# Waiting by semaphore for products in GpSimd's DMA queue, and another order of the last products, in a hybrid stick-breaking and retention layer

## The chip, the cores and the metric

One NeuronCore of one Trainium2 chip runs the whole program. The metric is the device time of one execution in microseconds, the median of several runs. Engines are named as in the profile: PE (TensorE, matrix products), PEld (its weight loads), DVE (VectorE), ACT (ScalarE), POOL (GpSimd, which here mostly issues DMAs and masks tiles), SP (the sync engine, which issues DMAs only). Every engine works through a queue of its own in order.

## The reference

One inference step of a layer with two groups of eight heads. 1024 frames of a new stream (the prompt) and 8 x 16 frames of running streams (the sample) are normalised and projected, one head group attends by stick-breaking, the other by retention; both outputs are normalised by head, multiplied with a gate, and go through one output projection. What the change touches is the end of it, on the prompt's rows:

```python
y = jnp.concatenate([y_sb, y_r], axis=-1)          # 2048 wide, both head groups
out = jnp.einsum('bte,ed->btd', y, w_out)          # output projection, 2048 x 2048
x = x + rms_norm(out, norm_post)                   # out / rms(out) * norm_post, added to the input
```

Beside it stand the new keys and values and the retention states.

## The kernel before

The prompt's 1024 rows are handled in two groups of four tiles of 128 rows; group 0 also carries the 128 sample rows. For each group and head the kernel projects q, k, v and gates (`products`, `project_rows`, `project_both`, L310 to L406), each weight block being split into a high and a low part in a format that PE takes (`split`, L139: ACT rounds, DVE subtracts) and multiplied in three products. The attention of a head runs beside it as a job: scores, sigmoids (ACT), masks (POOL, `weights`, L602), a scan (DVE, L616), a turn through DRAM (`turn_out`, `turn_in`, L569 and L581), products with the values, and a last norm and gate (`finish`, L634), whose result goes to DRAM (s_y) and, for group 1, is added by an adding DMA into the row sums S1 (L659).

The output projection multiplies the rows of both groups with w_out by a scheme with seven products in place of eight for blocks of rows and columns (as in Strassen's method). It needs sums of rows (S1, S2, s3, s4; in DRAM, made by `row_sums`, L1243, with copies and adding DMAs from DRAM to DRAM on POOL's queue) and sums of columns of w_out (s_t, `column_sums`, L1223, by DVE). The table `STEPS` (L281) lists the 28 products of this stage, each of 4 tiles x 4 blocks x 3 = 48 matmuls; (2, "1") is product 1 of the third of four quarter passes. Tile t and column block c of the result are gathered in `outs[t][c]` by `give` (L1394), which at the last contribution squares on ACT (for the norm) and multiplies with norm_post on DVE. The first four tiles are finished by `finish_first` and stored by `send_first` while the last products run; the other four are finished one by one by `last_done`, each after its last product: `last_scale` works out the factor, `scale` multiplies by it and adds x, `send` stores. The sum with x has two forms: for some (t, c) (`added`, L1424) x was copied to y before (`give_x`, L1442, on ACT's queue), ACT scales, and an adding DMA on POOL's queue stores; for the others x is loaded (`load_x`, L1429, POOL's queue), DVE scales and adds, and a plain DMA stores, on POOL's queue for tiles 0 to 3 and on SP's for 4 to 7.

The order is set by jobs: `tick` (L172) is called after every projection matmul group and lets at most one job go on whose time has come, so waits in the code (`yield 12`) count products. `place` (L163) ties an instruction to the product just issued, for its place in the order only, without a semaphore: an engine whose queue reaches it early runs it early. `row_sums(0)` handles heads 0 to 3 while the heads of group 1 are still projected, `row_sums(1)` heads 4 to 7 during the output projection. `mixed_last` (L1318) runs the last two products of `STEPS`, (3, "7") and (3, "4"), tile by tile: "7" and at once "4" into the same PSUM bank.

Of the kernel before, what the change touches and what calls it, by code (L numbers as in the profile page):

```python
# [12 lines left out]
ALU = mybir.AluOpType  # L13
# [6 lines left out]
H = 8  # L20
# [3 lines left out]
PT = 8  # L24
# [39 lines left out]
def tile_hybrid_step(  # L64
# [26 lines left out]
    nc = tc.nc  # L91
# [16 lines left out]
    def x_rows(t):  # L108
        return x_prompt[0, t * P : (t + 1) * P, :] if t < PT else xs_flat
# [25 lines left out]
    s_sum = {n: scr.tile([P, H, 512], F32, name=f"s_{n}") for n in ("S1", "S2", "s3", "s4")}  # L135
# [22 lines left out]
    clock = [0]  # L158
    phase = [0]
    product = [None]  # L160
    AFTER = mybir.DependencyInfo(mybir.DependencyClass.NoSync, mybir.DependencyReason.DATA)

    def place(inst):  # L163
        if product[0] is not None:
            tc.add_manual_dep(inst.ins, product[0].ins.name, AFTER, reason="placed behind a product")

    class Job:
        def __init__(self, steps, after=0):
            self.steps, self.at, self.done = steps, clock[0] + after, False
            jobs.append(self)  # L170

    def tick():  # L172
        clock[0] += 1
        for job in jobs:
            if job.at <= clock[0]:
                wait = next(job.steps, None)
                jobs.remove(job)
                if wait is None:
                    job.done = True
                else:  # L180
                    job.at = clock[0] + wait
                    jobs.append(job)
                return
# [224 lines left out]
    with ExitStack() as s1:  # L408
# [49 lines left out]
        with tc.tile_pool(name="p0", bufs=2) as p0, tc.tile_pool(name="p0s", bufs=1) as p0s, tc.tile_pool(  # L458
            name="p0p", bufs=4, space=PSUM
# [164 lines left out]
        class Out:  # L624
# [5 lines left out]
            def done(self, i):  # L630
                sq = op.tile([P, P], F32, name="sq", tag="sq", bufs=1)
                nc.scalar.activation(sq, self.o[:, i, :], AF.Square, accum_out=self.ssq[:, i : i + 1])
# [610 lines left out]
        def row_sums(q, wait):  # L1243
            heads = range(q * H // 2, (q + 1) * H // 2)
            for name, first, more in (
                ("S2", lambda h: s_sum["S1"][:, h, :], lambda h: s_y[0][:, h, :NB_TOK]),
                ("s3", lambda h: s_y[0][:, h, :NB_TOK], lambda h: s_y[1][:, h, :]),
                ("s4", lambda h: s_sum["S2"][:, h, :], lambda h: s_y[0][:, H + h, :NB_TOK]),
            ):
                for act, src in ((nc.gpsimd.dma_start, first), (add_rows, more)):  # L1250
                    for h in heads:
                        if not ready[h]():
                            while not ready[h]():
                                yield 3
                            yield 48
                        place(act(s_sum[name][:, h, :], src(h)))
                        yield wait
                made.add((name, q))

        made = set()  # L1260
        ready = {}

        def add_rows(dst, src):
            return nc.gpsimd.dma_start(dst, src, accum_op=ALU.add)
# [31 lines left out]
        def mixed_step(name, k, p, bank, block, fresh=False):  # L1296
            hi, lo = mix[USES[name]]
            wh, wl = block
            ts = slice(p * P, (p + 1) * P)
            for n, (a, b) in enumerate(((hi, wh), (hi, wl), (lo, wh))):  # L1300
                product[0] = nc.tensor.matmul(  # L1301
                    bank, a[:, k, ts], b,
                    start=(fresh and k == 0 and n == 0), stop=(k == H // 2 - 1 and n == 2),
                    skip_group_check=True,
                )
                tick()
# [11 lines left out]
        def mixed_last(two, banks, done):  # L1318
            kept = [mp.tile([P, 4, 512], F32R, name=f"w{x}", tag=f"m{x}1") for x in "hl"]
            blocks = [list(mixed_blocks(keep=kept)), list(mixed_blocks())]  # L1320
            for p in range(4):
                for name, w in zip(two, blocks):
                    for k in range(H // 2):
                        mixed_step(name, k, p, banks[p], w[k])
                    done(name, p)

        for gi in range(2):
            if gi:
# [47 lines left out]
    with ExitStack() as s3:  # L1376
# [11 lines left out]
        gpost = c3.tile([P, D], F32, name="gpost")  # L1388
# [2 lines left out]
        given = {(t, c): 1 for t in range(4) for c in range(2)}  # L1391
        xrs = {}

        def give(t, c, bank):  # L1394
            o = outs[t][c]
            n = given[t, c] = given.get((t, c), 0) + 1
            end = n == (4 if t < 4 else {0: 3, 1: 5, 2: 2, 3: 4}[c])
            if n == 1:
                nc.scalar.activation(o, bank, AF.Copy)
            elif end and t >= 4:  # L1400
                nc.vector.scalar_tensor_tensor(o, bank, -1.0, o, ALU.mult, ALU.subtract)  # L1401
            else:
                nc.vector.tensor_tensor(o, bank, o, ALU.add)  # L1403
            if end:
                sq = rp.tile([P, 512], F32, name="sq3", tag="sq3")
                nc.scalar.activation(sq, o, AF.Square, accum_out=ssq[:, t, c : c + 1])
                nc.vector.tensor_tensor(o, o, gpost[:, c * 512 : (c + 1) * 512], ALU.mult)  # L1407

        def scale(t, c, rs):
            o = outs[t][c]  # L1410
            if added(t, c):
                nc.scalar.activation(o, o, AF.Copy, scale=rs)
            else:
                nc.vector.scalar_tensor_tensor(o, o, rs, xrs[t, c], ALU.mult, ALU.add)  # L1414

        def send(t, c):
            at = y_rows(t)[:, c * 512 : (c + 1) * 512]
# [4 lines left out]
            return (nc.gpsimd if t < 4 else nc.sync).dma_start(at, outs[t][c])  # L1422

        def added(t, c):  # L1424
            return c < (2 if 4 <= t < 7 else 1)

        wanted = [(t, c) for t in range(PT) for c in range(4) if not added(t, c)]

        def load_x(q):  # L1429
            for x in "hl":  # L1430
                xr = mp.tile([P, 5, 512], F32, name="xr", tag=f"m{x}{q}")
                for j in range(5):
                    if wanted:
                        t, c = wanted.pop(0)
                        place(nc.gpsimd.dma_start(xr[:, j], x_rows(t)[:, c * 512 : (c + 1) * 512]))
                        xrs[t, c] = xr[:, j]
                        yield 10

        xs_given = {}
        SYNC = mybir.DependencyInfo(mybir.DependencyClass.Sync, mybir.DependencyReason.DATA)  # L1440

        def give_x():  # L1442
            for t in range(PT):
                cs = slice(0, 1024 if added(t, 1) else 512)
                xs_given[t] = nc.scalar.dma_start(y_rows(t)[:, cs], x_rows(t)[:, cs])
                place(xs_given[t])
                yield 24
# [32 lines left out]
        def send_first():  # L1480
            for n in range(16):
                while len(scaled) <= n:
                    yield 2
                place(send(*scaled[n]))
                yield 12 if added(*scaled[n]) else 8

        def finish_sample():
# [16 lines left out]
        scaled = []  # L1504
# [3 lines left out]
        for step, (n, name) in enumerate(STEPS):  # L1508
# [28 lines left out]
            def last_done(name, p):  # L1537
                t = 4 + p
                c = {"7": x2, "4": x1}[name]
                give(t, c, banks[3, "1"][p])  # L1540
                if name == "7":
                    more_of(t, c)
                else:
                    u_ = last_scale(t, c)
                    for cc in (0, 1, 3, 2):
                        scale(t, cc, u_)
                        send(t, cc)
# [99 lines left out]
```

## Time and profile before

| | |
|---|---|
| median of 3 runs | 2324.88 us (2320.08, 2324.88, 2325.47) |
| the profiled execution | 2320.76 us, its span 2319.0 us |
| granted PE clock, mean over the span | 0.996 |
| busy: PE, DVE, ACT, POOL | 2271.0, 1418.3, 918.6, 629.1 us |
| DMA | 476.21 MB, mean 205 GB/s |

The span reaches from the first to the last instruction of the profiled execution; the time of that execution is 1.76 us longer. Lines of the profile name source line, engine, operation and output<-inputs with buffer numbers left out, so s_S stands for S1 and S2, s_s for s3 and s4. An entry like [5.05 <-DMA s_S<-sg] gives the engine's idle time ahead of the row and what ended it.

### The profile page before, as it was taken

How to read it: one execution, taken by the hardware profiler on the slowest of the kernel's cores; microseconds unless marked ns; L12 is line 12 of the kernel's file. 1: busy time of each engine (PE TensorE's matmuls, PEld its weight loads, DVE VectorE, ACT ScalarE, POOL GpSimd, SP SyncE). 2: the span in 40 equal slices, each digit the busy share in tenths (PEclk: the TensorE clock that was granted, in tenths of full speed). 3: DMA queues.
4: the chain of work that ended last, by engine and by line, in shares of the span. 5: the costliest groups of instructions: out<-in, count | busy, mean ns of one | idle time of the engine just before them, and what ended most of it. 6: DMA issues, size and time to landing. Idle time of an engine off the chain costs nothing. (4 is left out here: it accounts for less than half of the span.)

```text
span 2319.0 us, 38754 instructions
## 1 busy us (share of the span) xinstructions
PE 2271.0 (98%) x13920; PEld 2012.8 (87%) x13920; DVE 1418.3 (61%) x2770; ACT 918.6 (40%) x1896; POOL 629.1 (27%) x930
## 2 busy tenths in 40 slices
PE   7999999999999999999999999999899999999996
PEld 7999999999999999999888888888788888888884
DVE  8246564556555564555757767676566656756766
ACT  6323332323333242333443444454334444545343
POOL 2123241414224141322412322142323213131022
PEclk9999999999999999999999999999999999999998
DMA  7659787797869787798968788888888776787566
GB/s 253 153 142 226 172 182 182 178 208 158 201 161 198 179 187 179 163 227 216 224 193 253 219 241 239 238 246 247 231 237 199 207 189 179 233 274 245 176 207 174
DMA packets 701185, 476.21 MB, mean 205 GB/s; under 512 B 232416, under 2 KB 631008, under 8 KB 699200
## 3 DMA queue, kind: packets, MB, share of 16 engines
q1 hardware_dynamic: 615968, 309.71, 51.3%
q0 software_dynamic: 48672, 140.69, 23.6%
q10 hardware_dynamic: 36352, 23.34, 3.4%
q8 instruction: 109, 1.79, 0.3%
q14 instruction: 84, 0.69, 0.1%
HBM read 371.89 MB, written 117.18 MB: 211 GB/s over the span
## 5 line engine op out<-in xcount | busy, mean ns | idle before, releaser
L315 PE MATMUL acc<-mh,wh 128*128 128x256 f32 (+2 forms) x2304 | 660.8, 339 | 5.7 <-DVE rv L1166 5.7
L315 PE MATMUL acc<-ml,wh 128*128 128x256 f32 (+2 forms) x2304 | 661.7, 340 | 0.8 <-DVE p0u L153 0.8
L315 PE MATMUL acc<-mh,wl 128*128 128x256 f32 (+2 forms) x2304 | 662.5, 340 | 0.0
L141 DVE TENSOR_TENSOR wl<-wr,wh 128x512 fp32r<-128x512 f32 x432 | 296.8, 690 | 414.8 <-ACT wh L140 400.8
L140 ACT ACTIVATE wh<-wr 128x512 fp32r<-128x512 f32 x432 | 272.8, 632 | 601.1 <-PE acc L315 354.4
L315 PEld LDWEIGHTS acc<-mh,wh 128*128 128x128 f32 x2304 | 421.8, 188 | 41.7 <-issue 6.6
L315 PEld LDWEIGHTS acc<-ml,wh 128*128 128x128 f32 x2304 | 421.5, 188 | 36.0 <-issue 6.6
L315 PEld LDWEIGHTS acc<-mh,wl 128*128 128x128 f32 x2304 | 421.5, 188 | 35.9 <-issue 8.2
L764 POOL DMA_DIRECT2D kc<-cache_sb_k x256 | 166.5, 655 | 283.1 <-DVE kcT L795 131.2
L374 PE MATMUL accn<-whn,mh 128*128 128x256 f32 x768 | 224.0, 292 | 0.0
L374 PE MATMUL accn<-wln,mh 128*128 128x256 f32 x768 | 217.2, 283 | 0.0
L374 PE MATMUL accn<-whn,ml 128*128 128x256 f32 x768 | 217.1, 283 | 0.0
L374 PEld LDWEIGHTS accn<-whn,mh 128*128 128x128 f32 x768 | 146.7, 191 | 9.8 <-issue 7.9
L374 PEld LDWEIGHTS accn<-wln,mh 128*128 128x128 f32 x768 | 146.8, 191 | 0.3
L374 PEld LDWEIGHTS accn<-whn,ml 128*128 128x128 f32 x768 | 146.6, 191 | 0.0
L616 DVE TENSOR_TENSOR_SCAN kp<-kp 128x640 f32<-128x640 f32 (+6 forms) x72 | 108.5, 1507 | 45.9 <-POOL kp L605 43.4
L1301 PE MATMUL a<-wl,mh 128*128 128x512 f32 x320 | 125.0, 391 | 0.8 <-DVE wl L141 0.8
L1301 PE MATMUL a<-wh,ml 128*128 128x512 f32 x320 | 125.0, 391 | 0.0
L1301 PE MATMUL a<-wh,mh 128*128 128x512 f32 x320 | 124.3, 390 | 0.4 <-DVE o L1403 0.4
L575 POOL DMA_DIRECT2D s_o<-so x16 | 18.6, 1162 | 302.8 <-DVE kp L594 227.8
L588 DVE STREAM_TRANSPOSE kp<-be 128x640 f32<-128x640 f32 (+6 forms) x72 | 95.5, 1326 | 5.9 <-DMA be<-s_bd 5.9
L141 DVE TENSOR_TENSOR wln<-wrn,whn 128x512 fp32r<-128x512 f32 x80 | 55.0, 689 | 68.2 <-ACT whn L140 67.6
(269 smaller groups left out, 3691.6 us busy)
## 6 DMA issues: line engine op xcount, KB each, us to landing
wr<-w_in SPq DMA_DIRECT2D x384, 256.0 KB, 4.7
vc<-cache_sb_v SPq DMA_DIRECT2D x64, 512.0 KB, 7.3
wr<-w_out SPq DMA_DIRECT2D x112, 256.0 KB, 4.3
wrn<-w_in SPq DMA_DIRECT2D x80, 256.0 KB, 3.8
kc<-cache_sb_k SPq DMA_DIRECT2D x256, 64.0 KB, 4.1
kc<-cache_sb_k POOLq DMA_DIRECT2D x256, 64.0 KB, 4.5
tr<-w_out SPq DMA_DIRECT2D x32, 512.0 KB, 6.1
s_t<-ts POOLq DMA_DIRECT2D x64, 256.0 KB, 4.6
```

The source lines that it names most:

```text
L140: nc.scalar.activation(hi, src, AF.Copy)
L141: nc.vector.tensor_tensor(lo, src, hi.bitcast(F32), ALU.subtract)
L315: last = nc.tensor.matmul(a[:, :m], lhs[:, j, :], rhs[w][:, j, o : o + m], start=(w == 0 and j == 0 and n == 0), stop=(w == KT // WQ - 1 a ...
L374: product[0] = nc.tensor.matmul(a, lhs[q][:, jj, ts], rhs[:, j, :], start=(w == 0 and j == 0 and n == 0 and t % 2 == 0), stop=(w == KT // ...
L575: place(q.dma_start(s[c].rearrange("m q a -> q m a"), src[:, 32 * c.start : 32 * c.stop].rearrange("q (m a) -> q m a", a=32),))
L588: place(nc.vector.transpose(dst.rearrange("p (k b j) -> p k j b", j=4, b=32), raw))
L616: nc.vector.tensor_tensor_scan(rev, rev, rev, 1.0, ALU.mult, ALU.bypass)
L764: (nc.gpsimd if i < 2 else nc.sync).dma_start(kc[32 * i : 32 * i + 32, :].rearrange("p (k d) -> p k d", d=32), cache_k[0, 2 * c + j, s * 5 ...
L1301: product[0] = nc.tensor.matmul(bank, a[:, k, ts], b, start=(fresh and k == 0 and n == 0), stop=(k == H // 2 - 1 and n == 2), skip_group_c ...
```

## The change

Five things are edited. `pace` ties a DMA to a product with a semaphore, so that POOL waits until PE has run that product; `passed` keeps the product of every tick. It replaces `place` for the copies and adds of the row sums (a product 40 ticks back for heads 0 to 3, the last one for heads 4 to 7), for the loads of x and for the first stores. A head's rows are taken up 60 ticks after its end was first seen. The last products go in steps over two tiles. The last multiplication with norm_post of the products "4" writes the PSUM bank in place of the SBUF tile. Tiles 6 and 7 lose the adding form: all their column blocks are scaled on DVE and stored by SP, so 24 blocks of x are loaded in place of 21, and x is copied to y for six tiles in place of eight.

```diff
+    def pace(inst, back=0):
+        tc.add_manual_dep(inst.ins, passed[-1 - back].ins.name, SYNC, reason="paced by a product")
+        return inst
+
     def tick():
         clock[0] += 1
+        if product[0] is not None:
+            passed.append(product[0])
...
                     for h in heads:
-                        if not ready[h]():
-                            while not ready[h]():
-                                yield 3
-                            yield 48
-                        place(act(s_sum[name][:, h, :], src(h)))
+                        while not settled(h):
+                            yield 3
+                        pace(act(s_sum[name][:, h, :], src(h)), 40 if q == 0 else 0)
                         yield wait
...
+        since = {}
+
+        def settled(h):
+            for g in ready:
+                if ready[g]():
+                    since.setdefault(g, clock[0])
+            return h in since and clock[0] - since[h] >= 60
...
-            for p in range(4):
-                for name, w in zip(two, blocks):
-                    for k in range(H // 2):
-                        mixed_step(name, k, p, banks[p], w[k])
-                    done(name, p)
+            for p, q in ((0, None), (1, 0), (2, 1), (3, 2), (None, 3)):
+                for name, w, tile_at in zip(two, blocks, (p, q)):
+                    if tile_at is not None:
+                        for k in range(H // 2):
+                            mixed_step(name, k, tile_at, banks[tile_at], w[k])
+                        done(name, tile_at)
...
-                nc.vector.tensor_tensor(o, o, gpost[:, c * 512 : (c + 1) * 512], ALU.mult)
+                gained[t, c] = bank if to_bank else o
+                nc.vector.tensor_tensor(gained[t, c], o, gpost[:, c * 512 : (c + 1) * 512], ALU.mult)
...
-                nc.vector.scalar_tensor_tensor(o, o, rs, xrs[t, c], ALU.mult, ALU.add)
+                nc.vector.scalar_tensor_tensor(o, gained[t, c], rs, xrs[t, c], ALU.mult, ALU.add)
...
-            return c < (2 if 4 <= t < 7 else 1)
+            return c < {4: 2, 5: 2, 6: 0, 7: 0}.get(t, 1)
...
-                        place(nc.gpsimd.dma_start(xr[:, j], x_rows(t)[:, c * 512 : (c + 1) * 512]))
+                        pace(nc.gpsimd.dma_start(xr[:, j], x_rows(t)[:, c * 512 : (c + 1) * 512]))
...
-            for t in range(PT):
+            for t in range(6):
...
-                place(send(*scaled[n]))
+                pace(send(*scaled[n]))
...
-                give(t, c, banks[3, "1"][p])
+                give(t, c, banks[3, "1"][p], name == "4")
```

The first place is POOL's queue while the fifth head of group 1 is handled: AFFINE_SELECT are the masks of a row, s_be and be the way of a row through DRAM, s_t the column sums, and s_S_109<-s_S_108 the copy of head 3's rows from S1 to S2. Before:

```order
L659 DMA s_S_108<-sg 128x512
L582 DMA be<-s_be_4_18204 128x5x128
L1256 DMA s_S_109<-s_S_108 128x512
L605 AFFINE_SELECT kp<-kp 128x128
L605 AFFINE_SELECT be<-be 128x128
L1240 DMA s_t_107<-ts 128x512
L1220 DMA s_raw<-raw 128x512
L1240 DMA s_t_107<-ts 128x512
L575 DMA s_be_6_18445<-be 128x28x32
L1264 DMA s_S_109<-s_y_104 128x512
L582 DMA be<-s_be_5_18327 128x6x128
```

With the change:

```order
L668 DMA s_S_108<-sg 128x512
L591 DMA be<-s_be_4_18202 128x5x128
L614 AFFINE_SELECT kp<-kp 128x128
L614 AFFINE_SELECT be<-be 128x128
L1249 DMA s_t_107<-ts 128x512
L1263 DMA s_S_109<-s_S_108 128x512
L1229 DMA s_raw<-raw 128x512
L1249 DMA s_t_107<-ts 128x512
L584 DMA s_be_6_18445<-be 128x28x32
L591 DMA be<-s_be_5_18325 128x6x128
L1249 DMA s_t_107<-ts 128x512 x2
L1278 DMA s_S_109<-s_y_104 128x512
```

The copy stands one row behind the masks and a store of s_t in place of directly ahead of the masks, and the add of S2 (from s_y) stands behind the load of be and two stores, in place of ahead of them.

The second place is the end of PE's queue: a_23436 (before) is the bank of the last tile, a_23434 and a_23433 (with the change) the banks of the last tile and of the one ahead; wh and wl without a number are the weights of product "7", those with a number the first block of weights of "4". Before:

```order
L1301 MATMUL a_23436<-wh,s3h 128x512
L1301 MATMUL a_23436<-wl,s3h 128x512
L1301 MATMUL a_23436<-wh,s3l 128x512
L1301 MATMUL a_23436<-wh_24122,a22h 128x512
L1301 MATMUL a_23436<-wl_24123,a22h 128x512
L1301 MATMUL a_23436<-wh_24122,a22l 128x512
```

With the change:

```order
L1315 MATMUL a_23434<-wh,s3h 128x512
L1315 MATMUL a_23434<-wl,s3h 128x512
L1315 MATMUL a_23434<-wh,s3l 128x512
L1315 MATMUL a_23433<-wh_24123,a22h 128x512
L1315 MATMUL a_23433<-wl_24124,a22h 128x512
L1315 MATMUL a_23433<-wh_24123,a22l 128x512
```

Before, the first row of "4" (a22h) follows the last row of "7" in the same bank; now it goes into the bank of the tile ahead, and the last tile's "4" comes twelve rows later.

The third place is the end of DVE's queue, from the addition of the last product on (o_2 with a bank a). Before:

```order
L1401 SCALAR_TENSOR_TENSOR o_2_21911<-a_23436,o_2_21911 128x512
L1407 TENSOR_TENSOR o_2_21911<-o_2_21911,gpost 128x512
L1457 SCALAR_TENSOR_TENSOR most<-ssq_21942,most 128x1
L1464 RECIPROCAL lastr<-lastr 128x1
L1465 SCALAR_TENSOR_TENSOR lastu<-lastr,most 128x1
L1466 SCALAR_TENSOR_TENSOR lastu<-lastu,lastr 128x1
L1414 SCALAR_TENSOR_TENSOR o_1_21932<-o_1_21932,lastu,xr 128x512
L1414 SCALAR_TENSOR_TENSOR o_3_21919<-o_3_21919,lastu,xr 128x512
L1414 SCALAR_TENSOR_TENSOR o_2_21911<-o_2_21911,lastu,xr 128x512
```

With the change (five more rows follow it, the last of the factor and the four scalings of the last tile):

```order
L1418 SCALAR_TENSOR_TENSOR o_2_21911<-a_23434,o_2_21911 128x512
L1481 RECIPROCAL lastr<-lastr 128x1
L1425 TENSOR_TENSOR a_23434<-o_2_21911,gpost 128x512
L1482 SCALAR_TENSOR_TENSOR lastu<-lastr,most 128x1
L1474 SCALAR_TENSOR_TENSOR most<-ssq_21942,most 128x1
L1483 SCALAR_TENSOR_TENSOR lastu<-lastu,lastr 128x1
L1432 SCALAR_TENSOR_TENSOR o_0_21938<-o_0_21938,lastu,xr 128x512
L1432 SCALAR_TENSOR_TENSOR o_1_21931<-o_1_21931,lastu,xr 128x512
L1432 SCALAR_TENSOR_TENSOR o_3_21918<-o_3_21918,lastu,xr 128x512
L1432 SCALAR_TENSOR_TENSOR o_2_21910<-a_23433,lastu,xr 128x512
L1481 RECIPROCAL lastr<-lastr 128x1
L1482 SCALAR_TENSOR_TENSOR lastu<-lastr,most 128x1
```

Before, three scalings follow the last addition. Now the third tile's factor and its four scalings stand behind that addition too, ahead of the last tile's.

More of the change, by code (lines that the diff above doesn't have):

```diff
@@ L170, in __init__ @@
             jobs.append(self)
+    SYNC = mybir.DependencyInfo(mybir.DependencyClass.Sync, mybir.DependencyReason.DATA)
+    passed = []
+    def pace(inst, back=0):
+        tc.add_manual_dep(inst.ins, passed[-1 - back].ins.name, SYNC, reason="paced by a product")
+        return inst
     def tick():
         clock[0] += 1
+        if product[0] is not None:
+            passed.append(product[0])
         for job in jobs:
@@ L1392, in tile_hybrid_step, with give @@
         xrs = {}
-        def give(t, c, bank):
+        gained = {}
+        def give(t, c, bank, to_bank=False):
             o = outs[t][c]
@@ L1439, in tile_hybrid_step @@
         xs_given = {}
-        SYNC = mybir.DependencyInfo(mybir.DependencyClass.Sync, mybir.DependencyReason.DATA)
         def give_x():
-            for t in range(PT):
+            for t in range(6):
                 cs = slice(0, 1024 if added(t, 1) else 512)
```

## The prediction

> **What bounds the kernel now.** I read the stages first, then whom TensorE (PE) waits for, then the timeline at the two places found. In the table of stages the columns are the stretch in us, its length, busy us and instruction count of PE, PEld, DVE, ACT and POOL, the granted clock, the DMA share and GB/s.
>
> ```profile
> 1500.00:1600.00 100.00, 100.00 (x475) 83.79 (x474) 68.69 (x112) 46.46 (x90) 31.67 (x44) 1.00 0.86 248
> 1600.00:1700.00 100.00, 91.87 (x431) 76.33 (x430) 61.64 (x108) 39.80 (x84) 27.69 (x37) 0.97 0.87 241
> 1700.00:1800.00 100.00, 100.00 (x479) 83.77 (x478) 68.61 (x129) 44.15 (x92) 33.24 (x41) 1.00 0.80 208
> ...
> 2000.00:2100.00 100.00, 99.62 (x437) 81.69 (x436) 59.09 (x99) 46.72 (x73) 29.29 (x43) 1.00 0.88 271
> ...
> 2250.00:2300.00 50.00, 44.10 (x176) 33.69 (x177) 39.97 (x80) 23.94 (x56) 11.41 (x18) 0.97 0.50 143
> 2300.00:2306.00 6.00, 4.39 (x18) 2.93 (x16) 5.71 (x15) 3.85 (x9) 2.30 (x4) 1.00 1.09 205
> 2306.00:2319.00 13.00, 0.00 (x0) 0.00 (x0) 4.31 (x10) 1.90 (x5) 2.53 (x3) 0.61 0.87 208
> ```
>
> PE is the bound: the stages around 1600 to 1700 are full. Time can only come from where PE stands still: 8.13 us in 1600 to 1700, 5.90 + 1.61 us in 2250 to 2306, and 13.0 us after its last product. The two longest of PE's waits there, in the view of whom it waits for (total us, times, longest):
>
> ```profile
> PE acc L315 <- DVE rv L1166: 5.7, 1, 5.7
> ...
> PE accx L402 <- DVE wlx L141: 1.7, 1, 1.7
> ```
>
> **The stall near 1650.** Three rows of POOL, one of DVE, one of PE, in order of cause; the bracket holds the idle time ahead and its releaser.
>
> ```profile
> 1624.21 0.93 POOL L659 DMA_DIRECT2D s_S<-sg  x1
> ...
> 1631.08 0.57 POOL L1256 DMA_DIRECT2D s_S<-s_S  x1 [5.05 <-DMA s_S<-sg]
> 1631.65 0.31 POOL L605 TENSOR_SCALAR_AFFINE_SELECT kp<-kp 128x128 f32<-128x128 f32 x1
> 1631.99 2.09 DVE L616 TENSOR_TENSOR_SCAN kp<-kp 128x896 f32<-128x896 f32 x1 [5.50 <-POOL kp L605]
> 1636.33 0.50 PE L402 MATMUL accx<-wlx,mh 128*128 128x512 f32 x1 [1.69 <-DVE wlx L141]
> ```
>
> A head's output is added into S1 at 1624.21; the copy of the same rows into S2 is the next but one in POOL's queue and waits 5.05 us for it. POOL works in order, so the masks (L605) of the next row come late, DVE's scan waits for them, the weight splits stand behind the scan, and PE waits 1.69 us. What POOL and the weight queue held back then starts at once (DMA issues of 1625 to 1645, median us to landing, then the page's median for the same load; then ACT, PE):
>
> ```profile
> wr<-w_in SPq DMA_DIRECT2D x3, 256.0 KB, 11.3
> s_S<-s_y POOLq DMA_DIRECT2D x2, 256.0 KB, 11.6
> wr<-w_in SPq DMA_DIRECT2D x384, 256.0 KB, 4.7
> 1651.90 0.63 ACT L140 ACTIVATE wh<-wr 128x512 fp32r<-128x512 f32 x1 [6.91 <-DMA wr<-w_in]
> 1653.64 0.80 PE L315 MATMUL acc<-mh,wh 128*128 128x512 f32 x1 [5.69 <-DVE rv L1166]
> 1656.80 0.41 PE L315 MATMUL acc<-mh,wl 128*128 128x512 f32 x1
> 1657.05 0.39 PE L315 MATMUL acc<-mh,wh 128*128 128x512 f32 x1
> ```
>
> A weight load takes 11.3 us instead of 4.7 among two adding DMAs; ACT waits 6.91 us for it with the evacuation (L1165, L1166) behind, and PE waits 5.69 us. Afterwards twelve products, two of them wide, take the 3.16 us from 1653.64 to 1656.80; at full clock (a wide product 0.23 us, from the last two rows; a narrow one half) they would take 1.6. So this one event costs 8.1 + 1.5 = **9.7 us**.
>
> **What the change does there.** The copy moves behind both masks, one s_t store and a longer settling time (60 ticks, before 48 only for a head found unfinished; a tick is one product, 0.23 us), and the adds of S2 move behind later be loads. The masks then wait only for the row ahead, so the 5.05 us at POOL go, and with them the bunch. The new semaphore of these rows names a product 40 back, 40 x 0.23 = 9.2 us earlier than the place of the row; behind it in POOL's queue stand masks, s_be stores and be loads, for which DVE's scans and PE's values wait. Against that, POOL's idle times between 1500 and 2000 end with results of DVE or ACT that belong to the products just run, so it shows no lead of 9 us. I cost it at nothing; bounds: nothing, and one more event of 9.7 us. I take 8.0 of 9.7 back, since some adding DMAs still fall in this stage.
>
> The other paced rows stand in the last stage, which begins near 2018: 24 more copies and adds, 24 x loads (21 before) and 16 first stores, all in POOL's queue, each held until PE reaches the product ahead of its place. Behind them in that queue stand the refills of PE's operands, which wait for PE to release the tile in any case, at the end of a step, that is later than any product named ahead of them. The copies are issued early now and are not on PE's path (the stage 2000 to 2100 has 0.38 us idle). Taken: nothing; bounds -0.4, and +2.06 (below, PE's longest gap of the tail) if one refill comes late. ACT's queue loses two copies of x to y; nothing waits for them.
>
> **The tail.** PE's gaps, the load and store rows around them, and the end:
>
> ```profile
> 2269.53 0.50 PE L1301 MATMUL a<-wl,a22h 128*128 128x512 f32 x1 [1.59 <-DVE wl L141]
> 2279.20 0.51 PE L1301 MATMUL a<-wh,s3h 128*128 128x512 f32 x1 [0.77 <-ACT wh L140]
> 2284.12 0.50 PE L1301 MATMUL a<-wl,s3h 128*128 128x512 f32 x1 [2.06 <-DVE wl L141]
> 2284.98 0.63 PE L1301 MATMUL a<-wl,s3h 128*128 128x512 f32 x1
> 2288.34 0.39 PE L1301 MATMUL a<-wl,s3h 128*128 128x512 f32 x1
> 2302.87 0.50 PE L1301 MATMUL a<-wh,a22h 128*128 128x512 f32 x1 [1.54 <-DVE o L1401]
> 2305.53 0.40 PE L1301 MATMUL a<-wh,a22l 128*128 128x512 f32 x1
> 2278.52 1.80 ACT L140 ACTIVATE wh<-wrt 128x512 fp32r<-128x512 f32 x3 [2.79 <-DMA wrt<-s_t]
> wrt<-s_t SPq DMA_DIRECT2D x3, 256.0 KB, 2.6
> wrt<-s_t SPq DMA_DIRECT2D x2, 256.0 KB, 6.3
> 2258.38 0.89 POOL L1419 DMA_DIRECT2D out<-o  x1 [16.32 <-ACT o L1412]
> 2270.44 1.27 POOL L1422 DMA_DIRECT2D out<-o  x2
> ```
>
> The sixteen first stores leave POOL between 2258 and 2271.7; loads of the last weights, 2.6 us before (issues of 2250 to 2258), take 6.3 us in 2266 to 2272. Paced, the stores leave every 8 or 12 ticks, 4 x 12 + 12 x 8 = 144 ticks = 33 us in all, of the 192 products that PE still has: the loads come some 3 us earlier. That covers 0.77 and most of 2.06 us (I take 2.2), and the slow clock after them: eight products from 2284.98 to 2288.34 in 3.36 us instead of 1.87, **1.5 us**. The 1.54 us at 2302.87 is the second product of a tile waiting until DVE has read the first from the same bank; another tile's 12 products (2.8 us) now stand between: **1.5 us**. The 1.59 us at 2269 stay: DVE is full there with the scalings, which don't move. Sum 5.2 us; bounds 1.5 (only the bank's wait goes) and 7.5 (the gaps of both rows of stages) + 1.5.
>
> The Trainium skill (TensorE: Matmul & The Clock Gate, Part 1: The HAM clock gate) has the clock halved only after an idle window of some 3.4 us. The longest gap ahead of the slow products is 2.06 us, so by it the slow products would not hang on them, the 1.5 us would stay, and the sum would come out 1.5 us longer. The rows put them right behind these gaps, which I follow.
>
> Against it stands the end, by the order of rows. DVE after the last product, now and before:
>
> ```profile
> L1407 DVE TENSOR_TENSOR o<-o,gpost 128x512 f32<-128x512 f32 x20 | 13.5, 689 | 1.9 <-ACT sq L1406 1.9
> L1414 DVE SCALAR_TENSOR_TENSOR o<-o,lastu,xr 128x512 f32<-128x512 f32 x9 | 6.3, 748 | 0.1
> L1401 DVE SCALAR_TENSOR_TENSOR o<-a,o 128x512 f32<-128x512 f32 x16 | 10.7, 686 | 2.8 <-PE a L1301 2.8
> 2307.78 0.69 DVE L1407 TENSOR_TENSOR o<-o,gpost 128x512 f32<-128x512 f32 x1 [0.85 <-ACT sq L1406]
> 2309.46 2.08 DVE L1414 SCALAR_TENSOR_TENSOR o<-o,lastu,xr 128x512 f32<-128x512 f32 x3
> ```
>
> Before, DVE ends at 2311.54, 5.6 us after PE's end at 2305.93. Now one addition (0.6, rows follow each other 0.09 faster than their length), one multiplication 0.6, eight scalings of 0.66 (both last tiles, all on DVE) and some 1.3 us of short rows: 7.8, so 2.2 later, the 0.85 us wait for ACT's square already taken out. No row writes PSUM from DVE. Bounds from rows: no dearer than in SBUF (L1401, reading PSUM, 686 ns, L1407 689 ns), or, by the dearest 512-wide row (748), 0.06 more each, 0.5 for eight. I take nothing.
>
> The Trainium skill (Perfetto Trace Analysis, Optimizing Scalar/DVE Operations) speaks against the change here: it gives VectorE about 60 ns of access overhead per instruction on SBUF and about 125 on PSUM. By it the eight last rows with a PSUM operand would cost an estimated 0.5 us more; the rows L1401 and L1407 show no such difference for reads.
>
> The stores give part back. DMA of 2290 to the end (share of 16 engines over 29 us):
>
> ```profile
> q0 software_dynamic: 1008, 1.84, 40.7%
> q1 hardware_dynamic: 1296, 2.36, 23.1%
> ```
>
> Seven adding stores took 40.7% of 29 us, 1.69 us each; nine plain ones 0.74 each: 18.5 us, so the DMA engines were full from 2300 on (share 1.09 in 2300 to 2306, 0.87 of the 13 us behind, which is 11.3 us, to about 2317). Three adding ones become plain: 15.7 us, though the first leaves one step later. The last store then waits less: 1.4 us gained (bounds 0 and 2.8). The three more x loads (0.74 us each) fall near 2245, where nothing waits. Half of the 2.8 us I count, since the end also hangs on DVE. Tail in all: 5.2 - 2.2 + 1.4 = **4.4 us**.
>
> **Sum**: 8.0 + 4.4 = 12.4 us, from the profiled execution's 2320.76 (span 2319.0 and 1.76 around it): 2308.4. The median of the three runs is 4.1 us above that execution. If the excess sits in the stall that goes, the median comes to 2308, if elsewhere, to 2312: **2310**; the rivals below carry the same 2 us, half of the excess.
>
> **Rivals.** (1) The stall only moves: the DMAs that bunch are as many as before, and another accident of the same kind stands at another row. For it: DMA share 0.87 in the stage; against it: 1500 to 1600 and 1700 to 1800 have 0.86 and 0.80 and no idle PE. Then only the tail counts: 2320.8 - 4.4 + 2 = 2318. Chance 0.17. (2) The tail gives nothing, DVE and the stores ending as late as now: 2320.8 - 8 + 2 = 2315, chance 0.13. (3) Slower: POOL, in order, meets a waiting copy before PE has reached its product, and the masks behind are late as at 1631. It decides where POOL is over 9.2 us ahead of PE, against which its waits above speak; each such block costs up to 9.7 us, two besides the present one, with the tail's gain, 2320.8 + 19.4 - 4.4 = 2336. Chance 0.08. (4) It does nothing: the semaphores are always passed and the order's shifts are noise, 2323, chance 0.07. That leaves 0.55 for the forecast, 2303 to 2317.
>
> What a measurement of this kernel can tell from no change is about 0.3%: below 2317.9 is faster, above 2331.9 slower. Faster: nearly all of the forecast (0.51), half of (1), most of (2): 0.70; slower 0.08; same 0.22. The range 2300 to 2325 leaves out (3) and a little on each side.
>
> **What would show it.** PE full in 1600 to 1700 and no POOL wait for s_S<-sg ahead of the masks shows the first step; weight loads there near 5 us. Stores of tiles 0 to 3 spread over some 33 us, no PE gap near 2279 to 2284 and none before the last products show the second; DVE ending 7 to 8 us after PE shows the cost. A PE wait of over 4 us behind POOL anywhere from 1570 to 1900 would prove it wrong.

## The result, and the profile after

| | before | changed |
|---|---|---|
| median | 2324.88 us (5 runs, 2320.08 to 2329.13) | 2312.94 us (5 runs, 2305.73 to 2314.40) |
| ratio, 95% interval | | 0.9941 [0.9918, 0.9964] |
| span of the profiled execution | 2319.0 us | 2312.5 us |

The change makes the kernel 11.9 us faster; 2310 was predicted, with 2300 to 2325 as the range. The two profiled executions differ by 6.5 us only. The stages of the changed kernel, with the columns of the prediction:

```profile
1600.00:1700.00 100.00, 95.57 (x447) 79.14 (x446) 63.37 (x114) 41.83 (x88) 28.84 (x38) 0.98 0.88 247
...
2100.00:2200.00 100.00, 97.86 (x423) 80.00 (x422) 66.40 (x96) 43.43 (x71) 6.23 (x11) 0.98 0.60 197
...
2250.00:2300.00 50.00, 45.92 (x193) 35.37 (x191) 43.65 (x87) 25.88 (x62) 13.41 (x20) 1.00 0.70 181
```

The stage around 1650 still has 4.4 us of idle PE (8.1 before), the one from 2100 has 2.1 (0.8 before), and the one from 2250 to 2300 has 4.1 (5.9 before). Whom PE waits for, in the changed kernel (total us, times, longest):

```profile
PE pd L843 <- DVE kp L597: 3.2, 3, 1.5
PE acc L324 <- DVE rv L1175: 2.9, 1, 2.9
```

The wait behind the evacuation (rv) fell from 5.7 to 2.9 us. The line pd (a product with values) has three waits, near 633, 768 and 1164; the profile of before had only the last of them, 0.6 us.

**Where the time went, stretch by stretch.** Three rows of PE stand in both kernels in the same order of work: the first product of the sample's output (sao), the first product of the output projection (a), and the first one with s3 among the last four products of `STEPS`, (2, "7"). Their starts before, and then in the changed kernel:

```profile
1395.57 0.39 PE L1213 MATMUL sao<-who,mh 128*128 128x512 f32 x1
1979.25 0.39 PE L1301 MATMUL a<-wh,mh 128*128 128x512 f32 x1
2250.66 0.47 PE L1301 MATMUL a<-wh,s3h 128*128 128x512 f32 x1 [0.92 <-DVE o L1403]
```

```profile
1397.64 0.39 PE L1222 MATMUL sao<-who,mh 128*128 128x512 f32 x1
1977.01 0.39 PE L1315 MATMUL a<-wh,mh 128*128 128x512 f32 x1
2249.86 0.39 PE L1315 MATMUL a<-wh,s3h 128*128 128x512 f32 x1
2299.66 0.40 PE L1315 MATMUL a<-wh,a22l 128*128 128x512 f32 x1
```

The differences of such starts, up to PE's end and the span's end, make five stretches (PE ends with the row of 2299.66, at 2300.06; before, at 2305.93). The order of the instructions is the same in both kernels up to the first of these rows, so what differs there is not the change's. The table has them for both kernels and for every run of the experiments below (us):

| profiled run | to sao | middle | output | tail | after PE | span |
|---|---|---|---|---|---|---|
| before | 1395.6 | 583.7 | 271.4 | 55.3 | 13.1 | 2319.0 |
| changed | 1397.6 | 579.4 | 272.9 | 50.2 | 12.4 | 2312.5 |
| e1_rows | 1396.7 | 576.9 | 270.8 | 53.8 | 14.2 | 2312.4 |
| e2_paced_tail | 1395.2 | 584.6 | 270.8 | 51.9 | 13.4 | 2315.8 |
| e3_two_tiles | 1396.2 | 586.2 | 269.9 | 51.8 | 15.9 | 2319.9 |
| e4_plain_stores | 1398.9 | 585.3 | 271.8 | 54.2 | 11.7 | 2321.9 |
| e5_after_again | 1394.9 | 579.8 | 271.0 | 49.7 | 12.6 | 2307.9 |
| e6_settled_only | 1395.3 | 577.9 | 270.2 | 49.7 | 12.2 | 2305.3 |
| e7_sbuf_mult | 1395.6 | 576.5 | 269.8 | 51.3 | 13.1 | 2306.4 |
| e8_scalings_spread | 1402.3 | 574.5 | 269.6 | 47.0 | 11.8 | 2305.2 |
| e9_two_tiles_plain | 1401.9 | 583.4 | 271.6 | 52.5 | 13.1 | 2322.5 |
| e10_paced_stores | 1397.9 | 586.5 | 272.8 | 52.1 | 13.5 | 2322.7 |
| e11_both | 1399.3 | 576.5 | 269.9 | 49.2 | 11.8 | 2306.7 |
| e12_act_shares | 1399.3 | 576.6 | 269.8 | 48.8 | 14.0 | 2308.5 |

The first column alone spreads over 7.4 us (1394.9 to 1402.3) with the same work in the same order. The middle separates cleanly: 583.4 to 586.5 in the six kernels without the new row sums, 574.5 to 579.8 in the eight with them; the means are 585.0 and 577.3, **7.7 us** apart. The tail is 5.1 and 5.6 us shorter in the two profiles of the changed kernel, the end behind PE 0.6 and 0.5.

**The middle, read in the changed kernel** (POOL, DVE, ACT, PE in order of cause):

```profile
1627.55 0.92 POOL L668 DMA_DIRECT2D s_S<-sg  x1
1628.11 1.24 POOL L591 DMA_DIRECT2D be<-s_be  x1
1631.04 0.29 POOL L614 TENSOR_SCALAR_AFFINE_SELECT kp<-kp 128x128 f32<-128x128 f32 x1 [1.68 <-ACT kp L608]
...
1634.87 0.55 POOL L1263 DMA_DIRECT2D s_S<-s_S  x1 [0.89 <-DMA s_S<-sg]
1631.36 2.02 DVE L625 TENSOR_TENSOR_SCAN kp<-kp 128x896 f32<-128x896 f32 x1 [1.02 <-POOL kp L614]
1649.19 0.63 ACT L140 ACTIVATE wh<-wr 128x512 fp32r<-128x512 f32 x1 [4.09 <-DMA wr<-w_in]
1650.93 0.50 PE L324 MATMUL acc<-mh,wh 128*128 128x512 f32 x1 [2.88 <-DVE rv L1175]
```

The masks now wait only for ACT, and the scan starts 1.02 us after DVE's last work instead of 5.50; PE's 1.69 us at the weight split is gone. The copy comes after the masks and waits 0.89 us with nothing urgent behind it. But the second half of the stall is still there, smaller. Loads issued from 1625 to 1645 in the changed kernel:

```profile
wr<-w_in SPq DMA_DIRECT2D x3, 256.0 KB, 8.8
```

They take 8.8 us (11.3 before, 4.7 as the page's median), ACT waits 4.09 us for one, with the evacuation behind it, and PE 2.88.

**The tail in the changed kernel**: PE's gaps, the first and the last of the sixteen first stores, the load of weights in the stretch 2266 to 2272, DVE's last row:

```profile
2265.92 0.50 PE L1315 MATMUL a<-wh,a22h 128*128 128x512 f32 x1 [0.87 <-DVE o L1418]
2268.45 0.50 PE L1315 MATMUL a<-wl,a22h 128*128 128x512 f32 x1 [1.32 <-DVE wl L141]
2280.50 0.50 PE L1315 MATMUL a<-wl,s3h 128*128 128x512 f32 x1 [1.05 <-DVE wl L141]
2285.34 0.47 PE L1315 MATMUL a<-wh,a22h 128*128 128x512 f32 x1 [0.84 <-DVE o L1418]
2257.29 0.90 POOL L1437 DMA_DIRECT2D out<-o  x1 [7.80 <-DVE o L1432]
2289.15 0.54 POOL L1440 DMA_DIRECT2D out<-o  x1 [1.09 <-PE a L1315]
2307.18 0.74 DVE L1432 SCALAR_TENSOR_TENSOR o<-a,lastu,xr 128x512 f32<-128x512 f32 x1
```

```profile
wrt<-s_t SPq DMA_DIRECT2D x4, 256.0 KB, 4.0
```

The stores spread over 32.4 us, the weight loads take 4.0 us instead of 6.3, the gap of 2.06 us has become 1.05, and the wait of 1.54 us in the last tile is gone. DVE ends at 2307.9, 7.9 us after PE; the last store lands 4.6 us later (7.5 before).

### The profile page after: what moved, and what is told of

Read it like the earlier page. It is cut to its first block, busy times and chain, and to the rows that moved or that the text cites. A ratio compares the mean times of both kernels' runs of the same rounds, so it can differ in the third digit from the quotient of the medians.

```text
span 2312.5 us, 38806 instructions
## 1 busy us (share of the span) xinstructions
PE 2268.9 (98%) x13920; PEld 2012.5 (87%) x13920; DVE 1420.5 (61%) x2773; ACT 919.9 (40%) x1895; POOL 627.7 (27%) x930
## 3 DMA queue, kind: packets, MB, share of 16 engines
q8 instruction: 109, 1.79, 0.3%
## 4 chain that ended last, share of the span: by engine, by line
PE 90%; DVE 4%; DMA 3%; ACT 1%; issue 1%; SPq 0%; POOL 0%; DVEq 0%; ACTq 0%
PE acc L324 50%; PE a L1315 12%; PE accn L383 11%; PE accx L411 4%; PE pa L721 3%; PE z L688 2%; PE sao L1222 2%; PE pd L857 1%; DMA be<-s_bd 1%; PE zc L792 1%; PE rs L879 1%; DMA wr<-w_in 1%; PE pS L912 1%; PE pa L897 1%; PE pa L902 1%
## 5 line engine op out<-in xcount | busy, mean ns | idle before, releaser
L584 POOL DMA_DIRECT2D s_o<-so x16 | 18.6, 1162 | 300.9 <-DVE kp L603 228.7
```

## The experiments

Medians are compared with runs of the kernel before on the same chip in the same job (2326.15, 2324.65 and 2328.01 us in the three jobs).

**The row sums alone.** Kernel before, with

```diff
+                        while not settled(h):
+                            yield 3
+                        pace(act(s_sum[name][:, h, :], src(h)), 40 if q == 0 else 0)
```

> The kernel before with the row sums' part alone: heads are taken up 60 ticks after their end, the copies and adds wait by semaphore for a product 40 back (heads 0 to 3) or the last one (heads 4 to 7). Theory A (the prediction's first step): the stall near 1650 goes, 8.0 us faster, PE's idle time in 1600 to 1700 falls from 8.1 us to under 1, the weight loads there land in about 5 us. Theory B (what the profile of the change suggests: the masks come in time, but the weight loads of 1640 still meet adding DMAs and other loads): about 4.5 us faster, 3 to 5 us of PE idle in that stage, weight loads of 8 to 9 us. Rival (the stall only moves): within 2 us of before.

Measured: 2317.66 us, 8.5 us faster (ratio 0.9958 [0.9941, 0.9975]); middle 576.9 us, PE idle 3.7 us in 1600 to 1700, a wait of 2.03 us behind the evacuation. The first step's size holds (8.0), though the picture of the stage is that of theory B. The two fit together in part because the row sums also remove a wait that the profile of before did not have. It stands near 1804 in all five other runs with the old row sums, 1.53 to 1.86 us long, and in none of the eight with the new ones. In the run e2_paced_tail, PE's row and then the DMA issues of 1787 to 1800:

```profile
1803.42 1.16 PE L721 MATMUL pa<-vn,kp 128*128 128x128 f32 x8 [1.58 <-DVE kp L597]
```

```profile
wr<-w_in SPq DMA_DIRECT2D x3, 256.0 KB, 6.8
s_s<-s_y POOLq DMA_DIRECT2D x1, 256.0 KB, 6.0
s_s<-s_S POOLq DMA_DIRECT2D x1, 256.0 KB, 6.2
```

An add into s3 and a copy into s4 leave back to back, and the weight loads take 6.8 us. The transposition that PE waits for (kp) stands in DVE's queue behind a weight split; that waited 5.25 us for ACT, and ACT 5.39 us for a load. The profile of before has the same pair, and loads of 7.1 us, without a wait of PE, so the pair does not always lead to one. In the changed kernel, issues of 1784 to 1798, there is one add and the loads take 4.9:

```profile
wr<-w_in SPq DMA_DIRECT2D x5, 256.0 KB, 4.9
s_s<-s_y POOLq DMA_DIRECT2D x1, 256.0 KB, 4.8
```

**The semaphores of the tail alone** (loads of x, first stores), and the first stores without the loads of x:

```diff
-                        place(nc.gpsimd.dma_start(xr[:, j], x_rows(t)[:, c * 512 : (c + 1) * 512]))
+                        pace(nc.gpsimd.dma_start(xr[:, j], x_rows(t)[:, c * 512 : (c + 1) * 512]))
-                place(send(*scaled[n]))
+                pace(send(*scaled[n]))
```

> The kernel before with the semaphores on the loads of x and the first stores alone. Theory A: the first stores spread over about 33 us, PE's gaps of 0.77 and 2.06 us near 2279 and 2284 shrink to under 1 us together and the slow clock behind them goes: 2.2 + 1.5 = 3.7 us faster. Rival (the sixteen first stores delay nothing that PE needs; the gaps hang on DVE, full with scalings): the gaps stay, within 1 us of before.

> The kernel before with the semaphores on the first stores alone, without those on the loads of x. Theory A (the profile's account of the run with both: PE's end 3.5 us earlier in the last 56 us, nothing elsewhere): PE's gaps near 2279 and 2284 under 1 us together, PE's stretch from 2250 to its end 3 to 4 us shorter. By the medians of the run with both: 8.7 us faster. If it is 3 to 4 us here, the rest of the 8.7 was the spread of the runs; if the loads of x had a share, this run is 2 us or more behind that one and PE's stretch of 2200 to 2250 shows it.

Measured: 2317.49 us with both, 8.7 us faster (0.9960 [0.9944, 0.9976]); 2324.43 with the stores alone, 3.6 faster (0.9981 [0.9970, 0.9992]). The tails agree, 51.9 and 52.1 us against 55.3. PE's gaps, and its wait for the bank, in e2_paced_tail:

```profile
2281.12 0.50 PE L1310 MATMUL a<-wl,s3h 128*128 128x512 f32 x1 [0.69 <-DVE wl L141]
2285.91 0.47 PE L1310 MATMUL a<-wh,a22h 128*128 128x512 f32 x1 [0.79 <-DVE o L1410]
2299.36 0.50 PE L1310 MATMUL a<-wh,a22h 128*128 128x512 f32 x1 [1.55 <-DVE o L1410]
```

So the stores did delay the weights. The 5 us by which the run with the x loads is ahead in its median have no place in the trace: it is ahead by 2.7 us before the first row sum, 1.9 in the middle and 2.0 in the output stage, all within what runs differ by. Whether the x loads' semaphores gain anything stays open.

**Two tiles in steps, plain stores, and both.** Kernel before with

```diff
+            for p, q in ((0, None), (1, 0), (2, 1), (3, 2), (None, 3)):
+                for name, w, tile_at in zip(two, blocks, (p, q)):
```

then with (x copied to y for six tiles, as in the change)

```diff
-            return c < (2 if 4 <= t < 7 else 1)
+            return c < {4: 2, 5: 2, 6: 0, 7: 0}.get(t, 1)
```

and then with both:

> The kernel before with the last products in steps over two tiles alone. Theory A: the 1.54 us that PE waits for the bank at the last tile go; against it two tiles now end within 2.8 us, so DVE and the adding stores end later after PE's last product by 0.5 to 1.5 us: between 1 us faster and no difference. Rival (DVE and the stores of two tiles collide at the end): 1 to 2 us slower, the time from PE's last product to the end grows from 13.0 to over 15 us.

> The kernel before with tiles 6 and 7 scaled on DVE and stored plainly (24 loads of x, 6 copies to y) alone. Theory A: the DMA engines are full from 2300 on, three adding stores less take 2.8 us of their time: 1.4 us faster, the time from PE's last product to the end falls from 13.0 to about 11.6 us. Rival (the end hangs on DVE): DVE has three scalings more, one of them behind the last product, 0.7 to 2 us slower.

> The kernel before with two edits that went alone above: the last products in steps over two tiles, and plain stores for tiles 6 and 7. Theory (the two-tile order takes 1.5 us from PE's end, and the 2.8 us that its end cost alone were adding stores on full DMA engines): PE's wait for the bank is gone and the time from PE's last product to the end is 12 to 13.5 us, about 2 us faster than before. Rival (the 2.8 us were DVE): 15 to 16 us from the last product to the end, no gain.

Measured: 2326.18 us, no change (0.9996 [0.9982, 1.0010]); 2323.87, 2.3 us less, which its interval does not tell from no change (0.9990 [0.9978, 1.0001]); 2325.65, 2.4 faster, barely clear of it (0.9988 [0.9977, 0.9999]). The trace is sharper. The new order takes PE's wait for the bank and makes the tail 2.0 us shorter than in e1_rows, whose tail has the old order, the same gaps and full clock (51.8 against 53.8); alone it gives that back behind PE's end (15.9 us against 13.1). Plain stores alone cut the end to 11.7. With both it is 13.1, so the loss of the order was the adding stores'. Whether the order gains anything beside plain stores is not shown: tail and end together take 65.5 us with both and 65.9 with plain stores alone, of which 1.7 are a slow stretch that the next paragraph takes up.

e3_two_tiles, e9_two_tiles_plain and e1_rows also tell something about the clock. All three have the gap of 2.06 us that the prediction blamed for the slow products, at a mean clock of 1.00 in the tail. e4_plain_stores has it at 2289.85 with full clock behind it, and its slow stretch elsewhere:

```profile
2274.88 0.59 PE L1301 MATMUL a<-wl,a22h 128*128 128x512 f32 x1 [1.33 <-DVE wl L141]
...
2289.85 0.50 PE L1301 MATMUL a<-wl,s3h 128*128 128x512 f32 x1 [2.07 <-DVE wl L141]
```

So the length of one gap does not decide. Its place does. In the fourteen traces the granted clock falls to one half sixteen times before PE's last product, for 3.41 us or twice that, and within a trace the starts and ends of these stretches lie whole multiples of 3.41 us apart. Cut into such steps (stretch, length, busy us and count of PE, clock, DMA share, GB/s), the surroundings of the gap in before, those of the same gap in e1_rows, and those of the slow stretch of e4_plain_stores are:

```profile
2281.45:2284.86 3.41, 1.35 (x6) 1.00 0.09 34
2284.86:2288.27 3.41, 3.41 (x10) 0.50 0.22 79
```

```profile
2277.75 0.50 PE L1315 MATMUL a<-wl,s3h 128*128 128x512 f32 x1 [2.07 <-DVE wl L141]
2272.95:2276.37 3.42, 2.50 (x9) 1.00 0.28 91
2276.37:2279.78 3.41, 2.03 (x9) 1.00 0.23 73
2279.78:2283.19 3.41, 3.41 (x16) 1.00 0.04 11
```

```profile
2271.73:2275.14 3.41, 1.46 (x5) 1.00 1.06 301
2275.14:2278.55 3.41, 3.41 (x9) 0.50 1.04 347
```

In before the gap lies in one step, in which PE stands still for 2.06 us, and the next step runs at half clock, which costs 1.7 us. In e1_rows the border of two steps cuts it; the two have 0.92 and 1.38 us of idle time, and the clock stays. In e4_plain_stores the gap of 1.33 us shares a step with most of one of 0.86. Over all fourteen traces every one of the sixteen stretches follows a step with at least 1.79 us of idle PE, and of the steps with more than that at full clock only two, of 1.81 and 1.82 us, had none behind them. Where the steps lie against the products differs from run to run, so for a gap of about 2 us it is chance.

**The changed kernel again, and without the semaphore of the row sums.** The first has no edit; the second

```diff
-                        pace(act(s_sum[name][:, h, :], src(h)), 40 if q == 0 else 0)
+                        place(act(s_sum[name][:, h, :], src(h)))
```

> The changed kernel once more, without an edit, timed in the same job as the three below and with a second profile. Additive theory (the parts give what they gave alone, by medians: rows 8.5, semaphores of the tail 8.7, two tiles 0, plain stores 2.3): about 19 us faster than before. Prediction: 14.9 us between the medians. First measurement: 11.9 us. If PE's waits near 633, 768 and 2181 of the first profile are chance, the second profile does not have them and ends 3 to 5 us earlier.

> The changed kernel with the semaphores taken off the row sums' copies and adds (they are only placed again; the settling over 60 ticks stays). Theory A (the move behind the masks does it, POOL has no lead of 9 us): within 1 us of the changed kernel, the copy of head 3 still behind the masks in time, PE idle in 1600 to 1700 as in the changed kernel (4 to 5 us). Rival (the semaphore does it): the copy is reached early again, PE idle there 7 us or more, 4 to 8 us slower than the changed kernel.

Measured: 2313.01 us (0.9954 [0.9936, 0.9972]) and 2310.32 (0.9943 [0.9926, 0.9961]). The gain of the whole is 11.6 us again and not the 19 us of the parts' medians added up. The second profile has no wait at 633 or 768, and its span is 4.6 us shorter than the first. Without the semaphore the middle is 577.9 us and the copy stands behind the masks just the same: the move by order did it. The semaphore has a price of its own, seen near 1670. POOL in the changed kernel, and PE's row that comes of it:

```profile
1660.72 2.28 POOL L614 TENSOR_SCALAR_AFFINE_SELECT be<-be 128x128 f32<-128x128 f32 x1
1669.01 0.84 POOL L1278 DMA_DIRECT2D s_S<-s_y  x1 [6.01 <-PE acc L324]
...
1670.17 1.29 POOL L591 DMA_DIRECT2D be<-s_be  x1
1687.26 1.16 PE L721 MATMUL pa<-vn,kp 128*128 128x128 f32 x8 [1.04 <-DVE kp L597]
```

The same place in e6_settled_only:

```profile
1658.31 2.29 POOL L614 TENSOR_SCALAR_AFFINE_SELECT be<-be 128x128 f32<-128x128 f32 x1
1660.54 0.87 POOL L1278 DMA_DIRECT2D s_S<-s_y  x1
...
1664.66 1.02 POOL L591 DMA_DIRECT2D be<-s_be  x1
```

The paced add holds POOL for 6.0 us, and the load of be behind it leaves 9.5 us after the mask instead of 6.4. In four of the five runs with the semaphore PE then waits 1.04 to 1.54 us here, in none of the three without. In the whole middle that cannot be told: the means are 577.4 with it and 577.0 without.

**The last multiplications back in SBUF.** The changed kernel with

```diff
-                give(t, c, banks[3, "1"][p], name == "4")
+                give(t, c, banks[3, "1"][p])
```

> The changed kernel with the last multiplications of the products 4 into the SBUF tile again. Theory A: each multiplication waits about 0.85 us for ACT's square of the same tile, so DVE ends some 8.7 us after PE's last product in place of 7.86 and the end comes 0.9 us later. Theory B (two tiles one behind the other: two such waits in a row): 1.5 to 2 us later. Rival (a PSUM operand costs VectorE more): each of the eight rows with one gets shorter by 0.06 us and the end does not come later.

Measured: 2310.95 us (0.9939 [0.9924, 0.9955]), which the runs cannot tell from the changed kernel; in the trace the end behind PE is 13.1 us instead of 12.2 to 12.6 (theory A, 0.9), and DVE ends 9.1 us after PE instead of 7.9. A multiplication in e7_sbuf_mult:

```profile
2293.39 0.69 DVE L1425 TENSOR_TENSOR o<-o,gpost 128x512 f32<-128x512 f32 x1 [0.85 <-ACT sq L1423]
```

**Scalings 8 ticks apart, alone and without the row sums' semaphore, and ACT's share at the end.**

```diff
-                    yield 4
+                    yield 8
```

The third kernel has e11_both and the table `{4: 2, 5: 2}`, so that tiles 6 and 7 have one adding block each.

> The changed kernel with the sixteen scalings of the first four tiles 8 ticks apart in place of 4 (their stores are 8 to 12 ticks apart in any case). Theory (PE's gaps near 2266 and 2268, 0.87 and 1.32 us, come from DVE, whose queue has eleven scalings in a row ahead of the weight splits): both gaps go below 0.5 us together, 1.5 to 2.2 us faster than the changed kernel. Rival (the loads of weights set them, since the first of them lands late): the gaps stay, and the stores, which come later, delay loads of weights further on: no gain or up to 2 us slower.

> The changed kernel with two edits that each did not lose alone: no semaphore on the row sums (settling kept), scalings of the first tiles 8 ticks apart. Theory: the gaps of 0.87 and 1.33 us near 2260 stay away, the middle as without the semaphore: 2307 to 2310 us, 3 to 5 us faster than the changed kernel. Rival (the differences among these runs were chance): 2311 to 2313.

> The kernel of the run before this one, and one column block each of tiles 6 and 7 scaled on ACT and stored by an adding DMA again (22 loads of x, 8 copies to y). Theory (after the change DVE, not the DMA engines, sets the end): DVE ends 0.7 to 1.3 us earlier after PE's last product, the end follows by 0.5 to 1.3 us. Rival (an adding store ends last): the time from PE's last product to the end grows from about 12 to 13 us or more, 1 us slower.

Measured: 2309.01 us (0.9932 [0.9917, 0.9946]), 2309.85 (0.9925 [0.9908, 0.9943]) and 2314.85 (0.9937 [0.9921, 0.9954]). In all three the gaps of 0.87 and 1.32 us near 2266 are gone, so they were DVE's, whose scalings stood in a row ahead of the splits. The tail is 47.0 us in the first; in the others a gap of 2.39 and 1.94 us at 2274 with a slow stretch behind it takes some back. The first two are the lowest medians of the study, 3 to 4 us below the changed kernel's, but the intervals of the ratios overlap, so that they beat it is likely and not shown. In e12_act_shares DVE ends 1.3 us earlier after PE, and yet the end comes 2.2 us later than in e11_both. The stores of its end, issues of 2297.5 to 2309, and then those of e11_both:

```profile
out<-o SPq DMA_DIRECT2D x6, 256.0 KB, 5.2
out<-o POOLq DMA_DIRECT2D x2, 256.0 KB, 6.1
```

```profile
out<-o SPq DMA_DIRECT2D x8, 256.0 KB, 2.8
```

Two adding stores among the last eight make the plain ones take 5.2 us instead of 2.8: the rival was right, and it is why the change needs the plain form there.

## Why the prediction was right, step by step

- **The middle, 8.0 us forecast, 7.7 measured as a mean (4.3 between the first two profiles).** That the copy ahead of the masks starts the stall was right: the masks come in time and PE's 1.69 us go. That the bunch behind goes with it, with weight loads near 5 us, was wrong: they take 8.8 us, and 0.9 to 2.9 us of wait behind the evacuation are left in the eight runs, in three of them (the two profiles of the changed kernel and e6_settled_only) with a slow stretch of 3.41 us behind it. By the busy times of PE, its idle time in the middle falls from 8.8 to 3.4 us on average, and what half clock costs there from 2.2 to 0.6; 0.8 us are not accounted for. Of the 5.4 us of idle time 1.4 are the wait near 1804, which the prediction could not see, since the one trace of before did not have it. So the stall itself gave some 5.5 us, and that the sum still came near 8 is partly luck. (The two rows from which the prediction takes 0.23 us for a wide product lie 0.25 us apart; those right behind them lie 0.22 and 0.24 apart, so the figure holds.) "I cost it at nothing", of the semaphore, was right for the sum, but not at its place (1.0 to 1.5 us near 1685).
- **The other paced rows, nothing.** Right for the output stage as a whole: means of 271.4 us in the six old kernels and 270.5 in the eight new ones. Of the loads of x alone it stays open.
- **The tail, 5.2 us forecast, 5.1 and 5.6 measured, one term of it by luck.** The gaps behind the stores (2.2 forecast) gave 1.8, from 53.8 in e1_rows to 51.9 and 52.1; the order (1.5) gave 2.0. The third term, "the slow clock after them", 1.5 us, is there in the profile of before (1.7) and gone in the tails of both profiles of the changed kernel, so the sum comes out. But the same gap has full clock behind it in four other runs, so the forecast counted as certain what is chance, and the medians hold only a part of it. The changed kernel has such stretches too: in its first profile one stands at 2181, behind a weight split (a step with 2.15 us of idle PE), and its output stage is 1.4 us longer than before's. By the rule of the Trainium skill that the prediction set aside (TensorE: Matmul & The Clock Gate, Part 1: The HAM clock gate) the clock is halved only after an idle window of some 3.4 us. The traces agree with the 3.4 us as the length of a step, but 1.79 us of idle time within one were enough. The prediction was right that the slow products hang on the gap, and could not know from one trace that this depends on where the gap falls.
- **The end, 0.8 us later forecast, 0.5 to 0.6 earlier measured.** DVE's part was exact: 7.9 us after PE, 7.8 forecast. The stores' part was mis-sized: "Half of the 2.8 us I count, since the end also hangs on DVE". The last store now lands 4.6 us after DVE instead of 7.5, so all of it came, 2.9, and 2.2 - 2.9 = -0.7 is about what was measured. The cost of a PSUM operand that the Trainium skill gives (Perfetto Trace Analysis, Optimizing Scalar/DVE Operations) does not show: the eight rows take 0.69 to 0.75 us each, as in SBUF.
- **The median.** "If the excess sits in the stall that goes, the median comes to 2308, if elsewhere, to 2312": it seems to sit elsewhere. The time up to the first row sum differs by up to 7.4 us between profiles of the same order, and before's profile was, at 1395.6, among the quickest. That is the likely reason why 2312.9 was measured and not 2310; the executions behind the medians have no traces to show it. The two profiled executions differ by only 6.5 us because the changed one lost 2.1 us before the change begins and 1.4 in the output stage.
- **The rivals.** (1), the stall only moves, was right in part: 0.9 to 2.9 us of it remain. (2) fell with the tail's 5 us. (3), POOL blocked by a paced row, occurs once, near 1685, at a ninth to a sixth of its price. (4) fell.

## What to carry to other kernels

Before a stall in one trace is priced, split two or more profiles at instructions that stand in all of them: stretches that the edit does not touch show how much is chance, and a stage's gain then shows at a fraction of what the medians need. An in-order queue that issues DMAs should not have a row that waits for a DMA, or for a semaphore, ahead of rows that other engines need; moving it in the order was enough here, and the semaphore only paid where nothing urgent stood behind it (the stores). Edits at the end of a kernel are to be judged together: the order of the last products shortened PE's tail by 2.0 us and lost it again behind PE's end as long as the slow adding stores stood there.

## What the hardware showed that was not expected

- The granted clock of PE falls to one half in stretches of 3.41 us (8 products of 0.43 us each in place of 0.23) or twice that, on steps of 3.41 us that are the same throughout a trace, after a step in which PE stood still for 1.79 us or more, in one gap or in several (0.86 and 1.33 us in e4_plain_stores). A gap of 2.06 us that the border of two steps cuts left the clock alone (e1_rows).
- The same order of instructions took from 1394.9 to 1402.3 us up to the same product, with PE waits for be's way back from DRAM of 0.6 us in one profile (0.6 at 1162, before) and 4.7 us in another (six waits, e8_scalings_spread, with a slow stretch behind the longest). All idle time of PE in this part ranges from 17.3 us (before) to 23.2 (e9_two_tiles_plain). Why the way back varies was not tried.
